# First loads of x and of the weights issued together on three queues, and the first squares on two engines, in an eight-core decoder layer

## The chip, the cores and the metric

The kernel runs on the 8 cores of one Trainium2 chip; every core works on one prompt and four sample rows. The metric is the time of the slowest core in device microseconds (us). Runs have a state: in the slow state one die (cores 0 to 3, or 4 to 7) has a clearly lower granted TensorE clock. Ratios and mean spans leave such runs out; a median of the table of runs is of all runs of that kernel, slow ones too. Small clock differences of a die remain; where they matter, the undisturbed cores are compared.

## The reference

One layer of a decoder. The part that this change touches is its very beginning, the first half-step FFN:

```python
def half_ffn(x, g, w_gate, w_up, w_down):
    h = rmsnorm(x, g)
    return (jax.nn.silu(h @ w_gate) * (h @ w_up)) @ w_down
...
xp = xp + 0.5 * half_ffn(xp, *ffn1)      # then attention, recurrence, memory, merge, second FFN
```

D_MODEL is 1024, D_FF is 2816, and a core has 2052 columns (tokens), cut into six tiles x0 to x5. Nothing can be multiplied before a tile's mean square is known, so the first matmuls wait for x, squares, a sum over 1024 rows and a scaling.

## The kernel before

Columns are tokens, rows are features: a tile x_k is 128 partitions x 8 chunks x n columns. Widths of the first three tiles are 352, 336 and 336.

```python
FT = [(0, 352), (352, 336), (688, 336), ...]      # first column, width

def load_x(k, src, parts=1, after=(), queues=(SP,)):
    w = 8 // parts                       # chunks in one DMA
    for q in range(parts):
        P.dma(queues[q % len(queues)], ... dst of chunks q*w .. , reads=list(after), writes=dx[k][q * w:(q + 1) * w])

def sq(k, c, late=1000.0, pair=True):    # first tiles: pair=False
    b = P.tile(brp)
    if not pair:
        actf(b, xv(k, c), AF.Square, [dx[k][c]], [b.d])                  # ScalarE
        mm(p, ones_n, b, c == 0, c == 7, ...)                            # sum over partitions, in PSUM
    ...
# rstd(k): Ln, then Exp on ScalarE -> 1/rms.   to_h(k, ...): hT = x * gain * rstd, 8 operations on VectorE

def gate_up(half, w, hook=None):
    for j in range(NJ):                                                  # 22 weight tiles of 128 x 2048
        b = load_w(w[j], 2048, first_w[min(j, 5)] if hook else ())       # on GpSimd's queue; waits for first_w
        for k in HT[half]:                                               # x0, x1, x2
            ... 8 matmuls gate, 8 matmuls up, Silu on ScalarE, product on VectorE

first_w = [dx[0][0:4], dx[0], dx[1][0:4], dx[1], dx[2][0:4], dx[2]]      # weight j waits for this part of x
```

The head of the program:

```python
load_x(0, xt, 4, queues=(SP, ACT))
... constants: ones_n, EPS, zero; then the gains (vecs, 128 rows of 208 bytes) on ScalarE's queue
for k in range(3):
    if k:
        load_x(k, xt, 2, after=dx[k - 1][0:5] if k == 1 else dx[k - 1][0:4])   # SyncE's queue only
    for c in range(8):
        sq(k, c, 0.0, False)
    to_h(k, rstd(k), gf1)
... four constants written by GpSimd (1.43 us), then gate_up(0, ...)
```

So x and weights take turns: x0, then w0 with x1, and so on. A list scheduler in the Python code decides, while the program is built, the order of instructions on each engine from a table of estimated costs (`DMA_RATE` is its estimate of each queue's rate). On the chip this order is fixed: an instruction that waits holds up everything behind it on its engine, ready or not (in e4 below, an Exp that was ready stood 8 us behind a square that was not).

The softmax here doesn't subtract the row's maximum and nothing guards it: scores larger than these inputs give would overflow.

## Time and profile before

| what | value |
|---|---|
| time, median of the first 3 runs | 1809.42 us (1807.29 to 1811.98) |
| slowest core of the profiled run | core 2, 1802.6 us |
| TensorE (PE) busy on it | 1738.2 us, 96% |
| matmuls in the first 60 us, by core 0 to 7 | 190, 166, 165, 190, 188, 175, 199, 169 (mean 180) |
| span + 0.143 us x that count, by core | 1825.8 to 1826.2 us |

A warm matmul of this stage starts 0.143 us after the one before it. Adding to each core's span the time of the matmuls that it finished in the first 60 us gives the same number for all eight cores within 0.4 us. So these cores differ only by what they did in the head, and a matmul gained there is 0.143 us gained at the end. I call the count N60.

The table by stretch for core 2, the slowest. In the brackets after each busy time is the number of instructions; the first bracket is TensorE's, and PEclk is the granted clock:

```profile
core 2: us, PE busy (x) PEld busy (x) DVE busy (x) ACT busy (x) POOL busy (x), PEclk, DMA share, GB/s
0.00:60.00 60.00, 33.07 (x165) 18.13 (x166) 16.16 (x35) 30.44 (x54) 7.33 (x20) 0.91 0.80 170
```

Core 2: 165 x 0.143 = 23.6 us of warm work in 60 us, so 36.4 us are lost. (The prediction below says 176 and 35: it added up windows of 5 us, which count a matmul that crosses a boundary twice. All counts from here on are of one window.)

The timeline of TensorE on core 2 (start, duration, operation, out<-in, count, and in brackets the idle time before it with what ended it). `hb` are the sums of squares, `ps` and `nd` the gate and up products; 352 columns is x0, 336 is x1 or x2:

```profile
10.27 3.80 PE L80 MATMUL hb<-br,cb 128*128 128x352 bf16 x8 [10.27 <-ACT br L80]
21.88 0.44 PE L80 MATMUL hb<-br,cb 128*128 128x336 bf16 x1 [7.81 <-ACT br L80]
...
23.06 0.79 PE L80 MATMUL ps<-hT,wp 128*128 128x352 bf16 x2
...
31.36 0.30 PE L80 MATMUL hb<-br,cb 128*128 128x336 bf16 x1 [3.67 <-ACT br L80]
...
43.58 0.72 PE L80 MATMUL ps<-hT,wp 128*128 128x336 bf16 x2 [3.79 <-DVE hT L80]
```

The first product (`ps`) comes at 23.06 us. What holds it back is the fixed order of ScalarE. There, the Exp that finishes 1/rms of x0 (the last line) stands behind a square of x1:

```profile
14.17 0.56 ACT L80 ACTIVATE fr<-hb,vec 128x352 f32<-128x352 f32 x1 [0.69 <-PE hb L80]
21.17 0.57 ACT L80 ACTIVATE br<-XA,vec 128x336 bf16<-128x336 f32 x1 [6.44 <-DMA XA<-xt]
21.65 0.57 ACT L80 ACTIVATE fr<-fr,vec 128x352 f32<-128x352 f32 x1
```

The Ln of x0 was done at 14.7 us, and w0 had landed at about 15.3 us (issued at 8.11, 7.2 us to landing); the Exp waited for x1. All eight cores show it: the Exp starts 0.5 us after that square (at 15.4 to 21.7 us), the first product 1.4 us after the Exp, and, by and large, the later x1 came, the smaller is the count of the core in the table above (199 on core 6, where x1 came first, 165 on core 2, where it came last).

Two matmuls in 0.59 us (23.06 to 23.65) is the slow rate; the Trainium skill (TensorE: Matmul & The Clock Gate, Part 1) tells of half rate until some 3.4 us of activity, and this trace agrees with 0.28 to 0.29 us a matmul after a long gap and 0.143 us once it is warm. The slow stretch from 43.58 us lasted 5.6 us here, with a granted clock of 0.50 in the records; in the first one, from 23.06 us, the records show 1.00, though the spacing is the same. The waits of TensorE on core 2 in the first 60 us (us in total, times, longest):

```profile
PE hb L80 <- ACT br L80: 22.9, 5, 10.3
PE ps L80 <- DVE hT L80: 3.8, 1, 3.8
```

ScalarE's squares are named, but they wait for x in their turn; the chain of waits of the same core says so (start, duration, what):

```profile
1.51 7.51 DMA XA<-xt
9.09 11.99 DMA XA<-xt
```

x0 took 7.5 us and x1 12.0 us. In the first 3 us of these 12 nothing of x1 moved, and then it shared the engines with w0 and w1. From 9 to 12 us almost nothing moved at all, as the DMA view of 9 to 12 us shows (queue, packets, MB written, share of the time of 16 DMA engines; q0 is GpSimd's weights, q1 SyncE's and q10 ScalarE's queue):

```profile
DMA packets 21, 0.09 MB, mean 29 GB/s; under 512 B 0, under 2 KB 0, under 8 KB 21
## 3 DMA queue, kind: packets, MB, share of 16 engines
q0 software_dynamic: 21, 0.09, 39.1%
```

### The profile page before, as it was taken

The page shows a single profiled execution, that of the slowest core. Times are in us where ns is not written, and L with a number is a line of the kernel's source. Part 1 is how long each engine was busy: PE and PEld are TensorE (multiplying, and loading weights), DVE is VectorE, ACT ScalarE, POOL GpSimd, SP SyncE. Part 2 cuts the span into 40 slices and gives each one's busy share as a digit, 9 for nine tenths or more (in the row PEclk, how much of TensorE's full clock was granted, in tenths as well). Part 3 has the DMA queues.
Part 4 walks back from the last instruction along what each step waited for, and adds up shares of the span by engine and source line. Part 5 has one row for each costly group of instructions (what it writes and reads, how often), then busy time and mean ns, then how long its engine had stood idle before and what let it go on. Part 6 is the DMA issues. An engine that isn't in the chain of part 4 may idle for free.

```text
span 1802.6 us, 33178 instructions; the slowest of 8 cores (1797.5 to 1802.6 us)
## 1 busy us (share of the span) xinstructions
PE 1738.2 (96%) x12105; PEld 1109.0 (62%) x12171; DVE 674.7 (37%) x1391; ACT 730.4 (41%) x1266; POOL 405.2 (22%) x543
## 2 busy tenths in 40 slices
PE   4999999999999999999999999999999999999996
PEld 1666666666655545555556566666666666666663
DVE  2223314222142435756576533543452221422213
ACT  5334414222145566758776633433342221322212
POOL 1112221001244051433431122322220002100021
PEclk9999999999999999999999999999999999999998
DMA  8486459656688554654547745596875447899562
GB/s 196 80 167 127 70 102 197 123 122 127 120 211 199 142 120 77 122 98 93 96 100 152 170 80 88 106 193 130 164 147 87 69 104 145 163 192 171 104 141 96
DMA packets 89391, 234.00 MB, mean 130 GB/s; under 512 B 32912, under 2 KB 40336, under 8 KB 86416
## 3 DMA queue, kind: packets, MB, share of 16 engines
q0 software_dynamic: 40608, 127.03, 44.6%
q1 hardware_dynamic: 46224, 59.26, 10.4%
q10 hardware_dynamic: 2400, 45.57, 8.7%
q8 instruction: 102, 1.67, 0.4%
q14 instruction: 57, 0.47, 0.1%
HBM read 321.27 MB, written 80.51 MB: 223 GB/s over the span
## 4 chain that ended last, share of the span: by engine, by line
PE 90%; DVE 3%; ACT 3%; issue 2%; DMA 1%; POOL 1%; DVEq 0%; ACTq 0%; SPq 0%; POOLq 0%
PE ps L80 49%; PE nd L80 33%; PE hb L80 8%; DVE XB L80 1%; ACT fr L80 1%; DMA XA<-xt 1%; DVE hT L80 1%; DVE br L80 1%; ACT br L80 0%; ACT L80 0%; ACT XA L80 0%; DVE fr L80 0%; POOL XA L80 0%; DVE XA L80 0%; POOL fr L80 0%
## 5 line engine op out<-in xcount | busy, mean ns | idle before, releaser
L80 PE MATMUL ps<-hT,wp 128*128 128x336 bf16 (+4 forms) x3839 | 637.2, 312 | 5.7 <-DVE hT L80 3.8
L80 PEld LDWEIGHTS ps<-hT,wp 128*128 128x128 bf16 x3856 | 365.6, 98 | 208.3 <-issue 6.4
L80 PE MATMUL nd<-hT,wp 128*128 128x336 bf16 (+4 forms) x2547 | 434.5, 312 | 1.4 <-ACT fr L80 0.2
L80 PEld LDWEIGHTS nd<-hT,wp 128*128 128x128 bf16 x2560 | 243.3, 98 | 134.7 <-issue 2.0
L80 ACT ACTIVATE fr<-ps,vec 128x336 f32<-128x336 f32 (+3 forms) x269 | 150.1, 560 | 343.8 <-PE ps L80 343.4
L80 PE MATMUL ps<-actb,wp 128*128 128x336 bf16 (+2 forms) x1612 | 253.8, 308 | 0.3 <-DVE XB L80 0.3
L80 PEld LDWEIGHTS ps<-actb,wp 128*128 128x128 bf16 x1612 | 157.3, 98 | 76.7 <-issue 0.6
L80 ACT ACTIVATE fr<-nd,vec 128x336 f32<-128x336 f32 (+3 forms) x185 | 103.4, 560 | 235.5 <-PE nd L80 235.2
L80 DVE TENSOR_TENSOR actb<-ps,fr 128x336 bf16<-128x336 f32 (+2 forms) x160 | 81.9, 514 | 266.2 <-PE ps L80 260.9
L80 PE MATMUL nd<-actb,wp 128*128 128x336 bf16 (+2 forms) x1076 | 173.0, 308 | 0.7 <-ACT fr L80 0.7
L80 POOL TENSOR_TENSOR fr<-fr 128x512 f32<-128x512 f32 (+3 forms) x96 | 108.0, 1132 | 161.0 <-DVE fr L80 140.2
L80 POOL DMA_DIRECT2D wp<-wgu x88 | 47.4, 538 | 400.3 <-PE ps L80 229.9
L80 PEld LDWEIGHTS nd<-actb,wp 128*128 128x128 bf16 x1076 | 105.0, 98 | 52.3 <-issue 1.0
L80 POOL TENSOR_TENSOR br<-fr 128x336 bf16<-128x336 f32 (+2 forms) x84 | 77.3, 923 | 181.2 <-ACT fr L80 181.0
L80 DVE TENSOR_TENSOR actb<-nd,fr 128x336 bf16<-128x336 f32 (+2 forms) x104 | 53.2, 513 | 173.2 <-PE nd L80 167.2
L80 ACT ACTIVATE fr<-XB,vec 128x352 f32<-128x352 f32 (+2 forms) x96 | 53.9, 577 | 138.5 <-DVE XB L80 138.5
L80 PE MATMUL hb<-hT,wp 128*128 128x512 bf16 (+1 forms) x514 | 95.2, 312 | 1.0 <-ACT fr L80 0.2
L80 ACT ACTIVATE fr<-XA,vec 128x336 f32<-128x336 f32 (+1 forms) x72 | 40.9, 578 | 130.2 <-DVE XA L80 130.2
L80 POOL DMA_DIRECT2D wp<-wd x64 | 34.8, 544 | 249.6 <-PE ps L80 128.5
L80 PE MATMUL hb<-br,cb 128*128 128x336 bf16 (+7 forms) x188 | 48.5, 300 | 28.9 <-ACT br L80 22.9
L80 ACT ACTIVATE fr<-fr,vec 128x512 f32<-128x512 f32 (+3 forms) x105 | 72.6, 700 | 5.0
L80 DVE SCALAR_TENSOR_TENSOR fr<-fr,ps 128x336 f32<-128x336 f32 (+2 forms) x85 | 43.2, 510 | 77.6 <-ACT fr L80 77.6
(244 smaller groups left out, 1630.9 us busy)
## 6 DMA issues: line engine op xcount, KB each, us to landing
wp<-wgu POOLq DMA_DIRECT2D x88, 512.0 KB, 8.9
wp<-wd POOLq DMA_DIRECT2D x64, 352.0 KB, 5.8
wp<-w_gb POOLq DMA_DIRECT2D x48, 384.0 KB, 8.8
wp<-w_hqf POOLq DMA_DIRECT2D x16, 512.0 KB, 8.3
vd<-br SPq DMA_DIRECT2D x48, 128.0 KB, 4.0
XA<-vd SPq DMA_DIRECT2D x12, 512.0 KB, 5.7
wp<-w_qk POOLq DMA_DIRECT2D x12, 512.0 KB, 7.6
pv<-fr SPq DMA_DIRECT2D x21, 256.0 KB, 6.4
```

The lines of the kernel that those rows point to most:

```text
L80: return f(*[g(x) for x in a], **{n: g(x) for n, x in k.items()})
```

## The change

The intent is to let nothing wait that need not: all of x0, x1 and x2 is issued at once on two queues, weights at once on the third, and squares go to whichever of ScalarE and VectorE the scheduler expects to be free. The scheduler gets one estimated rate for the first 20 us, 105 for every queue in place of 130 (SyncE), 190 (GpSimd) and 100 (ScalarE).

```diff
+    HEAD = 20000.0
+    HEAD_RATE = 105.0
...
-                    pipe[e] = max(pipe[e], start + issue) + o["nbytes"] / self.DMA_RATE[e]
+                    t = max(pipe[e], start + issue)
+                    pipe[e] = t + o["nbytes"] / (self.HEAD_RATE if t < self.HEAD else self.DMA_RATE[e])
...
+    def sq_first(k, c):
+        ...
+        P.op((ACT, DVE), (lambda e: e.activation(out=b.t[:, 0:n], in_=x, func=AF.Square, bias=zeroc, scale=1.0),
+                          lambda e: e.tensor_tensor(out=b.t[:, 0:n], in0=x, in1=x, op=ALU.mult)), reads=[dx[k][c], dc], writes=[b.d])
+        mm(p.t[:, 0:n], ones_n, b.t[:, 0:n], c == 0, c == 7, [b.d, dc], [p.d])
...
-            b = load_w(w[j].rearrange("p a c n -> p (a c n)"), 2048, first_w[min(j, 5)] if hook else ())
+            b = load_w(w[j].rearrange("p a c n -> p (a c n)"), 2048)
...
-    first_w = [dx[0][0:4], dx[0], dx[1][0:4], dx[1], dx[2][0:4], dx[2]]
...
-    load_x(0, xt, 4, queues=(SP, ACT))
+    P.dma(ACT, lambda e: e.dma_start(out=vec[:, 0:52], in_=vecs), writes=[dc])
+    for k in range(3):
+        load_x(k, xt, 4, queues=(SP, ACT))
...
-    P.dma(ACT, lambda e: e.dma_start(out=vec[:, 0:52], in_=vecs), writes=[dc])
     for k in range(3):
-        if k:
-            load_x(k, xt, 2, after=dx[k - 1][0:5] if k == 1 else dx[k - 1][0:4])
         for c in range(8):
-            sq(k, c, 0.0, False)
+            sq_first(k, c)
         to_h(k, rstd(k), gf1)
-    P.op(POOL, lambda e: e.memset(ones_b, 1.0), writes=[dm])      # and three more, moved to j == 5 of the weight loop
```

A part that adds filler matmuls in TensorE's idle time is in the diff as well, but it is never switched on (`fill` stays None).

More of the change, by code (lines that the diff above doesn't have):

```diff
@@ L183 @@
     WAIT = 1200.0
+    HEAD = 20000.0
+    HEAD_RATE = 105.0
+    fill, fill_end, FILL = None, 0.0, 80.0
     def __init__(self, nc, lanes=None):
@@ L384, in schedule @@
                 table = o["aset"]
+            if e == PE and order[PE] and self.fill is not None and start < self.fill_end:
+                o["fill"] = max(0, int((start - free[e] - 150.0) / self.FILL))
             o["t0"] = start
@@ L488, in body @@
                     for o in order[name]:
+                        for _ in range(o.get("fill", 0)):
+                            self.fill(e)
                         for s, k in o["waits"]:
@@ L722, in sq @@
             mm(p.t[:, 0:n], ones_n, b.t[:, 0:n], c == 1, c == 7, [b.d, dc], [p.d], late=late)
+    def sq_first(k, c):
+        n = FT[k][1]
+        if c == 0:
+            pss[k] = P.tile(psS)
+        p, b, x = pss[k], P.tile(brp), xv(k, c)
+        P.op((ACT, DVE), (lambda e: e.activation(out=b.t[:, 0:n], in_=x, func=AF.Square, bias=zeroc, scale=1.0),
+                          lambda e: e.tensor_tensor(out=b.t[:, 0:n], in0=x, in1=x, op=ALU.mult)), reads=[dx[k][c], dc], writes=[b.d])
+        mm(p.t[:, 0:n], ones_n, b.t[:, 0:n], c == 0, c == 7, [b.d, dc], [p.d])
     def rstd(k):
@@ L1359, in bulk_at @@
         return 1760e3
-    load_x(0, xt, 4, queues=(SP, ACT))
-    P.op(POOL, lambda e: e.memset(vec[:, 60:61], 1.0), writes=[d_one])
+    P.dma(ACT, lambda e: e.dma_start(out=vec[:, 0:52], in_=vecs), writes=[dc])
+    for k in range(3):
+        load_x(k, xt, 4, queues=(SP, ACT))
+    P.op(DVE, lambda e: e.memset(vec[:, 60:61], 1.0), writes=[d_one])
     P.op(ACT, lambda e: e.activation(out=vec[:, 63:64], in_=vec[:, 60:61], func=AF.Ln), reads=[d_one], writes=[d_one])
@@ L1367, in build_nc @@
     P.op(DVE, lambda e: e.memset(vec[:, 62:63], 0.0), writes=[dc])
-    P.dma(ACT, lambda e: e.dma_start(out=vec[:, 0:52], in_=vecs), writes=[dc])
     for k in range(3):
-        if k:
-            load_x(k, xt, 2, after=dx[k - 1][0:5] if k == 1 else dx[k - 1][0:4])
         for c in range(8):
-            sq(k, c, 0.0, False)
+            sq_first(k, c)
         to_h(k, rstd(k), gf1)
-    P.op(POOL, lambda e: e.memset(ones_b, 1.0), writes=[dm])
-    P.op(POOL, lambda e: e.memset(ones_h, 1.0 / 128), writes=[dm])
-    P.op(POOL, lambda e: e.memset(rst, 1.0), writes=[dm])
-    P.op(POOL, lambda e: e.memset(cb[:, 896:1408:64], 0.0), writes=[dm])
     for q, (src_, dst_) in enumerate(bulk):
@@ L1386, in hook @@
         elif j == 5:
+            P.op(POOL, lambda e: e.memset(ones_b, 1.0), writes=[dm])
+            P.op(POOL, lambda e: e.memset(ones_h, 1.0 / 128), writes=[dm])
+            P.op(POOL, lambda e: e.memset(rst, 1.0), writes=[dm])
+            P.op(POOL, lambda e: e.memset(cb[:, 896:1408:64], 0.0), writes=[dm])
             P.dma(ACT, lambda e: e.dma_start(out=cf[:, :], in_=cstf), reads=d_memT, writes=[dm])
```

## The prediction

> **What bounds the kernel now.** TensorE is busy 1738 of 1802.6 us (page, slowest core) and is 90% of the chain that ended last. The change touches only the first 45 us. There the timeline of core 2 shows the first ones-matmul at 10.3 us and the first real one at 23.06; the waits view puts 22.9 us on ACT squares (which wait for x) and 3.8 on hT. The windows table counts 176 matmuls in the first 60 us: at the warm spacing (0.143 us for 336 columns) 25 us of work, so 35 us were lost. Core 6 counts 208 (30 lost) and its span is 5.1 us shorter: head losses reach the end one for one. Cores 1, 2, 5, 7 all count 170 to 177. Part of the loss is clock: after a gap matmuls come 0.28 us apart for 4 to 6 us. The Trainium skill (TensorE: Matmul & The Clock Gate, Part 1) describes this, half rate until some 3.4 us of activity; the trace agrees.
>
> **Why the head is slow.** x and weights go in turn: w0 is issued at 8.1 us, x1 (two halves) at 9.1, only after x0, landing at 21.1 and 23.9; x2 at 21.1, landing at 28.8 and 32. From 9 to 12 us almost nothing moves (DMA windows). When busy, q0 writes 0.08 MB (reads 0.16) and q1 0.11 per us: 270 to 300 GB/s read.
>
> **What the change does.** All of x (4.19 MB) and seven weights (1.05 MB each) are issued from 1 us on. This adds no bandwidth: the Trainium skill (DMA: Bandwidth & Descriptors, Issuing engines are not separate DMA queues) says that they share 16 engines and interleave. The trace agrees: x1 needed 12 us while w0 and w1 ran. Estimate: x gets 155 GB/s of 270, so x0 lands later than now (8.5 us), at 12.5; w0 at 12.6, x1 21.5, w1 22, x2 30. After the last x0 squares come one more matmul, Ln, Exp and hT (0.56 us each): first real matmul at 16.5 instead of 23.1 us. Squares on two engines save about 1 us per tile, where the whole tile has landed. Moving POOL's memsets (1.43 us) lets weights go first. The filler code is never switched on. The changed rate only reorders instructions.
>
> **Sum, slow core.** Lost: 15.3 us around the first sums, 2.3 cold clock on w0 x0, 4 waiting for h of x1 (order is fixed in advance), 2.3 cold clock again, 0.5 other: 24.5 instead of 35.5 us. Gain 11 us; after 60 us nothing changes but small reordering (3 us either way).
>
> **Prediction.** 1809.4 - 11 = 1798 us, range 1791 to 1805. Faster by over 2%: 0.02; within 2%: 0.96; slower by over 2%: 0.02.
>
> **What shows it right or wrong.** x0 lands later than 8.6 us, first ps matmul between 14 and 18 us, hT of x2 complete before 37 us; matmuls in the first 60 us rise to about 245 on the slow cores, fewer at 0.28 us; the spread of cores shrinks. Windows from 100 us on look as before.
>
> **What would make it wrong.** If weights crowd out x (q0 started 4 us before q1 at 10 us although issued together), x0 lands at 15 us or later and the gain is 5. If the order fits the arrivals, the gain is 15. A reshuffle of the attention stage could add or take several us. Table switches (1.28 us) between Silu and Ln may stay in the chain of x1 and x2.

## The result, and the profile after

| | before | after |
|---|---|---|
| time of the first comparison, median of 4 | 1809.26 us (1807.29 to 1811.98) | 1804.57 us (1803.54 to 1805.91) |
| ratio of the fast runs | | 0.9973, 95% interval 0.9956 to 0.9991 |
| a second session on another chip, medians (of the fast runs alone 1805.51 and 1801.13) | 1805.79 us | 1801.27 us, ratio 0.9973 (0.9955 to 0.9991) |
| mean span of the eight cores there, fast runs | 1801.1 us | 1798.0 us |
| slowest core there, mean of the fast runs | 1804.2 us | 1799.6 us |
| N60 by core, profiled run | 165 to 199, mean 180 | 187 to 196, mean 191 (second session: 182 to 197, mean 192) |

A ratio is the mean time of one kernel's fast runs over that of the other's in the same rounds, so it is not quite the ratio of the medians.

The gain is 4.7 us where 11 were predicted, though the time itself lies in the predicted range. In the second session it splits into 3.1 us for the mean core and 1.5 us for a smaller distance from the mean core to the slowest. In the first comparison the cores 4 to 7 had a mean clock of 0.990 and were 3 to 4 us longer than their N60 says (core 0, at 0.992, 2 us); in the second they had 0.992 to 0.993 and only core 4 stood out, by 1.5 us. So that low clock is no steady part of the change.

The same views after, for core 4, the slowest of the profiled run (1802.0 us). By stretch:

```profile
core 4: us, PE busy (x) PEld busy (x) DVE busy (x) ACT busy (x) POOL busy (x), PEclk, DMA share, GB/s
0.00:60.00 60.00, 36.46 (x190) 20.13 (x191) 22.67 (x50) 23.41 (x41) 7.22 (x19) 0.89 0.79 170
```

The timeline of TensorE:

```profile
...
15.59 1.21 PE L80 MATMUL hb<-br,cb 128*128 128x352 bf16 x3 [4.76 <-ACT br L80]
18.69 4.85 PE L80 MATMUL ps<-hT,wp 128*128 128x352 bf16 x16 [1.89 <-DVE hT L80]
23.33 0.98 PE L80 MATMUL hb<-br,cb 128*128 128x336 bf16 x5
26.89 1.46 PE L80 MATMUL hb<-br,cb 128*128 128x336 bf16 x4 [2.58 <-ACT br L80]
31.47 1.47 PE L80 MATMUL hb<-br,cb 128*128 128x336 bf16 x4 [3.12 <-ACT br L80]
...
36.25 0.48 PE L80 MATMUL ps<-hT,wp 128*128 128x336 bf16 x1
```

The first product came 4.4 us earlier, at 18.69 us, 1.4 us after the Exp of x0 (17.27 us), which in the new order no longer stands behind a square of x1. But after w0 on x0 was done at 23.3 us, TensorE had only 15 sums to do until 36.25 us. Those sums are of x1 and of x2 alike: in the fixed order, all eight sums of x2 stand ahead of the products of x1. The waits:

```profile
PE hb L80 <- ACT br L80: 14.7, 6, 4.8
PE hb L80 <- DVE br L80: 6.9, 1, 6.9
PE ps L80 <- DVE hT L80: 1.9, 1, 1.9
```

ScalarE of the same core shows where the squares were (a line with [.. <-DMA XA<-xt] waited for x), with table loads and the Silu between them:

```profile
14.86 1.07 ACT L80 ACTIVATE br<-XA,vec 128x352 bf16<-128x352 f32 x2 [5.21 <-DMA XA<-xt]
...
26.18 1.04 ACT L80 ACTIVATE br<-XA,vec 128x336 bf16<-128x336 f32 x2 [5.25 <-DMA XA<-xt]
27.23 1.28 ACT L80 ACT_TABLE_LOAD   x1
28.53 0.55 ACT L80 ACTIVATE fr<-ps,vec 128x352 f32<-128x352 f32 x1
...
31.81 1.28 ACT L80 ACT_TABLE_LOAD   x1
33.11 0.54 ACT L80 ACTIVATE fr<-hb,vec 128x336 f32<-128x336 f32 x1
34.37 0.57 ACT L80 ACTIVATE br<-XA,vec 128x336 bf16<-128x336 f32 x1 [0.72 <-DMA XA<-xt]
34.85 0.56 ACT L80 ACTIVATE fr<-fr,vec 128x336 f32<-128x336 f32 x1
```

The last quarter of x0 reached ScalarE at 14.9 us (before, x0 was there at 9 us), that of x1 at 26.2 us, that of x2 at 34.4 us. The Exp of x1 (the last line) stood behind a square of x2. The chain of waits of the first 60 us on this core has one piece in place of the two of before:

```profile
4.58 29.71 DMA XA<-xt
```

And this is what the queues did from 10 to 12 us:

```profile
DMA packets 139, 0.45 MB, mean 223 GB/s; under 512 B 0, under 2 KB 0, under 8 KB 139
...
q0 software_dynamic: 47, 0.19, 59.0%
q10 hardware_dynamic: 47, 0.13, 22.8%
q1 hardware_dynamic: 45, 0.12, 21.3%
```

The three queues took turns packet by packet: 47, 47 and 45. The Trainium skill (DMA: Bandwidth & Descriptors, Queues, rings and completion order) says that each DMA engine goes round the queues "at *packet* granularity", and the counts agree. But the turns are not equally long. A weight packet held an engine for 0.590 x 16 x 2 us / 47 = 0.40 us, a packet of x (0.228 + 0.213) x 16 x 2 us / 92 = 0.153 us. So x, with two queues of three, had 44% of the engines' time and 0.125 MB per us, 125 GB/s.

### The profile page after: what moved, and what is told of

Read it like the earlier page. It is cut to its first block, busy times and chain, and to the rows that moved or that the text cites. A ratio compares the mean times of both kernels' runs of the same rounds, so it can differ in the third digit from the quotient of the medians.

```text
span 1802.0 us, 33181 instructions; the slowest of 8 cores (1797.7 to 1802.0 us)
## 1 busy us (share of the span) xinstructions
PE 1741.6 (97%) x12105; PEld 1109.3 (62%) x12171; DVE 681.7 (38%) x1404; ACT 722.9 (40%) x1252; POOL 404.5 (22%) x542
## 4 chain that ended last, share of the span: by engine, by line
PE 91%; DVE 3%; ACT 2%; issue 2%; DMA 2%; POOL 1%; ACTq 0%; DVEq 0%; POOLq 0%
PE ps L80 50%; PE nd L80 33%; PE hb L80 8%; DMA XA<-xt 2%; DVE XB L80 1%; ACT fr L80 1%; DVE br L80 1%; DVE hT L80 0%; ACT br L80 0%; ACT XA L80 0%; ACT L80 0%; DVE fr L80 0%; ACTq L80 0%; POOL XA L80 0%; DVE XA L80 0%
## 5 line engine op out<-in xcount | busy, mean ns | idle before, releaser
L80 PE MATMUL ps<-hT,wp 128*128 128x336 bf16 (+3 forms) x3829 | 633.9, 312 | 3.5 <-DVE hT L80 1.9
L80 PE MATMUL nd<-hT,wp 128*128 128x336 bf16 (+3 forms) x2557 | 435.3, 312 | 2.1 <-issue 0.9
L80 ACT ACTIVATE fr<-ps,vec 128x352 f32<-128x352 f32 (+3 forms) x276 | 154.0, 560 | 350.8 <-PE ps L80 350.5
L80 ACT ACTIVATE fr<-nd,vec 128x336 f32<-128x336 f32 (+3 forms) x178 | 99.6, 560 | 231.6 <-PE nd L80 231.1
L80 PE MATMUL hb<-br,cb 128*128 128x336 bf16 (+7 forms) x188 | 47.9, 305 | 27.8 <-ACT br L80 14.7
## 6 DMA issues: line engine op xcount, KB each, us to landing
wp<-wgu POOLq DMA_DIRECT2D x88, 512.0 KB, 10.4
```

Of the source, the lines that this page charges most:

```text
L80: return f(*[g(x) for x in a], **{n: g(x) for n, x in k.items()})
```

## The experiments

All kernels gave correct results. Every one was timed in 3 rounds against the kernel before; what is compared is the ratio, N60 and the arrival times. Two theories stood against each other:

- **Data.** Weights issued at once take the DMA engines from x, so x1 and x2 land late and TensorE starves.
- **Order.** The data would do, but the fixed order, made from a wrong estimate of rates, puts sums and squares of x2 ahead of the products and the Exp of x1.

| run | N60 mean (range) | median us | ratio to before (95%) |
|---|---|---|---|
| r1_after, the changed kernel | 192 (182 to 197) | 1801.27 | 0.9973 (0.9955 to 0.9991) |
| e1_order | 177 (173 to 182) | 1808.69 | 1.0014 (0.9998 to 1.003) |
| e3_weights_wait | 237 (221 to 247) | 1795.36 | 0.9941 (0.9925 to 0.9957) |
| e4_vecs_late | 181 (175 to 185) | 1801.96 | 0.9977 (0.9956 to 0.9999) |
| e2_act_squares | 181 (168 to 189) | 1801.91 | 0.9969 (0.9954 to 0.9984) |
| e5_old_order_held | 227 (213 to 235) | 1795.54 | 0.9935 (0.992 to 0.995) |
| e6_new_order_at_once | 201 (196 to 205) | 1798.54 | 0.9953 (0.9938 to 0.9968) |
| e9_best | 250 (243 to 263) | 1792.28 | 0.9917 (0.9901 to 0.9934) |
| e10_memsets_first | 188 (182 to 198) | 1807.25 | 0.9982 (0.9945 to 1.0018) |
| e11_best_held | 244 (239 to 249) | 1800.53 | 0.9928 (0.9907 to 0.9949) |
| e12_best_vecs_late | 260 (256 to 263) | 1804.52 | 0.9917 (0.9885 to 0.9949) |
| r2_best, e9_best again | 256 (243 to 262) | 1807.18 | 0.9928 (0.9908 to 0.9948) |

The last four lines need a warning: e10, e11, e12 and r2 ran in sessions in which cores 0 to 3 had a clock of 0.982 to 0.994 even in fast runs, and the kernel before took 1813.85 us (e10, e11) and 1821.27 us (e12, r2) there. Their medians are not to be set beside those above; the cores 4 to 7 of these sessions are, at 0.991 to 0.996 (in r2 cores 6 and 7 of the profiled run were still 5 us longer than their N60 says). Five of the medians include one or two slow runs; of the fast runs alone they are 1801.13 (r1), 1801.75 (e4), 1798.85 (e11), 1804.31 (e12) and 1806.30 us (r2).

### r1_after: the changed kernel again

> The changed kernel again, on the same chip as the next three. Every theory: ratio 0.997 to before; on the slow cores the second block of real matmuls (hT of x1) starts at 36 us, the last quarter of x0 lands at 14.7 us, the last of x2 at 34. It also shows whether the lower granted clock of die 1 (0.990 against 0.993) comes with the change or not: if it comes with the change, die 1 shows it here too and before doesn't.

Measured: N60 mean 192, ratio 0.9973, the same as the first time on another chip. The last squares of x0 began at 14.3 to 15.8 us, the first product at 18.2 to 19.7, the second block at 35.9 to 37.0 us. Die 1 had the clock of die 0 here, so its lower clock in the first comparison does not come with the change. One of its four runs was slow (2123 us).

### e1_order: the order alone

The scheduler is told rates nearer to the measured ones. The transfers stay as they are.

```diff
-    HEAD = 20000.0
-    HEAD_RATE = 105.0
+    HEAD = 36000.0
+    HEAD_RATE = {SP: 63.0, ACT: 63.0, POOL: 190.0}
...
```

> The changed kernel, with only the transfer rates that fix the instruction order made lower for x (63 GB/s on each of the two x queues for the first 36 us, 190 on the weights' queue), so that Exp of x1 stands ahead of the squares of x2 on ScalarE and the sums of x2 come after the first matmuls on hT of x1. Same transfers. Theory order (the wait for hT of x1 is made by the squares and sums of x2 placed ahead of it): landings unchanged (14.7, 26, 34 us), second block starts at 30 to 31 us instead of 36, 30 more matmuls in the first 60 us, 4 to 5 us faster than the changed kernel. Theory data (x arrives too late, whatever the order): second block still at about 36 us, no gain. Theory vecs: no gain.

Measured: a miss, and a useful one. The products of x1 did begin at 30.7 us in place of 36.3, as expected. But N60 fell to 177 and the ratio to before was 1.0014. The timeline of TensorE on core 4 shows a new wait in place of the old one:

```profile
30.68 0.44 PE L80 MATMUL ps<-hT,wp 128*128 128x336 bf16 x1 [3.40 <-DVE hT L80]
...
42.51 0.44 PE L80 MATMUL ps<-hT,wp 128*128 128x336 bf16 x1 [3.40 <-DVE hT L80]
```

hT of x2 was needed at 39 us and came at 42.5: its last squares (37.62 us) now stood behind two Silus and a table load on ScalarE, and its Ln (40.48 us) behind one more. The wait had only been moved to another place in the order. Some cores lost time much later as well. On core 7 the merge stage (1100 to 1300 us) waited for one weight, which the same core did not do in the profile of the changed kernel:

```profile
PE nd L80 <- DMA wp<-w_gb: 4.7, 1, 4.7
```

So this order, made for later arrivals, gave nothing while the arrivals stayed late. That no order could is not shown by it: part of the new wait is again order, and e6 below gains a little with late data.

### e3_weights_wait: the data alone, with a new order

x stays issued at once on two queues, and the rule `first_w` of before is put back, so weight 0 waits for the first half of x0 and so on.

```diff
-            b = load_w(w[j].rearrange("p a c n -> p (a c n)"), 2048)
+            b = load_w(w[j].rearrange("p a c n -> p (a c n)"), 2048, first_w[min(j, 5)] if hook else ())
+    first_w = [dx[0][0:4], dx[0], dx[1][0:4], dx[1], dx[2][0:4], dx[2]]
```

> The changed kernel, but each of the first six weights waits for the part of x that it waited for before the change (x is still issued at once). Theory data (the weights take the bandwidth that x needs): x0 lands at about 11 us instead of 14.7, x2 at about 22 instead of 34, second block of real matmuls at 25 to 27 us, 4 us or more faster than the changed kernel, although w0 lands later (15 to 17 us). Theory order: x2 lands earlier and so do its squares, so the wait behind them shrinks as well and the gain is about the same; the two are told apart by the run with the order alone. If SWDGE starts late and w0, w1 come too late, first real matmul at 20 us or more and no gain.

Measured: N60 237 and 1795.36 us, 5.9 us better than the changed kernel in the same session, and 10.4 us better than the kernel before. So x at once with the new order, without the weights at once, gave nearly the 11 us that were forecast for the whole change. With x alone in the queues, from 8 to 12 us on core 4:

```profile
q1 hardware_dynamic: 259, 0.62, 50.3%
q10 hardware_dynamic: 259, 0.64, 48.1%
```

That is 1.26 MB in 4 us, 315 GB/s for x instead of 125. The last squares of x0 began at 11.2 us (core 4) instead of 14.9. w0 came later, so the first product came later too, but products of x1 could follow at once:

```profile
20.84 1.06 PE L80 MATMUL ps<-hT,wp 128*128 128x352 bf16 x3
...
25.50 0.31 PE L80 MATMUL ps<-hT,wp 128*128 128x336 bf16 x1
```

The first product was 2.2 us later than in the changed kernel (w0 came later than the expected 15 to 17 us), the first of x1 10.7 us earlier. A gap of 13 us in the middle had been traded for 2 us at the start.

### e5_old_order_held and e6_new_order_at_once: the two crossed

In e3 the scheduler saw the waits, so the order changed too. These two runs separate that. In e5 the waits are added after the order is made, so that every engine has the changed kernel's order to the letter; in e6 the order is e3's to the letter and the waits are dropped afterwards.

```diff
         order = self.schedule()
+        for o in self.all:                         # e5: add the waits of the weights now
+            if o.get("hold"):
+                o["preds"] |= o["hold"]
+                o["t0"] += 1500.0
+            # e6 instead: o["preds"] -= o.get("drop", set())
```

> The instruction order of the changed kernel on every engine, kept to the letter, with the weights' issues held behind x as in e3_weights_wait (added after the order was made). So far span = 1825.1 us - 0.143 x (matmuls in the first 60 us) on every undisturbed core. Theory data: what counts is that x lands early; second block of real matmuls at 28 to 30 us instead of 36, 230 to 245 matmuls in the first 60 us (the changed kernel 192, e3_weights_wait 237), 1791 to 1797 us. Theory order: as the changed kernel, 185 to 200 matmuls, 1800 to 1802 us.

> The instruction order of e3_weights_wait to the letter, with all weights issued at once as in the changed kernel. Theory data: x2 lands at 34 us again, so about the changed kernel's loss: 185 to 205 matmuls in the first 60 us, 1799 to 1803 us. Theory order: as e3_weights_wait, 230 to 240 matmuls, 1794 to 1796 us.

Measured, N60 mean, and in brackets the mean span of the eight cores over the fast runs:

| | weights at once | weights wait for x |
|---|---|---|
| the changed kernel's order | 192 (1798.0 us) | 227 (1792.3 us) |
| e3's order | 201 (1796.5 us) | 237 (1791.5 us) |

Holding the weights is worth 35 or 36 matmuls in either order, that is 5.0 and 5.2 us by the count and 5.7 and 5.0 us by the spans. The order is worth 9 or 10 matmuls, 1.3 to 1.5 us by the count and 1.5 and 0.8 us by the spans. This settles the question between the theories: the weights that crowd x out are the main cause, the order a smaller one.

How small is less sure. The four kernels ran in two sessions (r1 and e3 on one chip, e5 and e6 on another, both undisturbed). Set against the mean span of the kernel before in the same session (1801.1 and 1801.7 us), holding is worth 6.3 and 4.3 us and the order 2.1 and 0.1 us. And in e6 GpSimd writes its constants first, so its weights start 1.3 us later than in the changed kernel and x0 and x1 land some 2 us earlier; so a part of what the first column puts down to the order may be data.

The gap that matters is the one between the products of x0 and of x1. In e5, in the changed kernel's order to the letter, it lies on core 4 between these lines:

```profile
26.12 2.11 PE L80 MATMUL hb<-br,cb 128*128 128x336 bf16 x9
...
32.51 0.48 PE L80 MATMUL ps<-hT,wp 128*128 128x336 bf16 x1
```

That is 6.39 us with 15 sums in it, so 4.2 us are lost, where the changed kernel with the weights at once lost 10.8. The expectation for e5 was a little too high: the second block began at 30.5 to 32.5 us instead of 28 to 30, and N60 is 227 instead of 230 to 245. e6 fell in the range of theory Data by N60 (185 to 205) and half a us below it in time (1799 to 1803).

In e5 the price of holding is plain to see. The waits of TensorE on core 4 in the first 60 us:

```profile
PE ps L80 <- DMA wp<-wgu: 8.4, 1, 8.4
...
PE hb L80 <- ACT br L80: 5.4, 6, 1.8
```

The squares of ScalarE are hardly waited for any more (5.4 us in place of 14.7), and the wait has become one for w0, 8.4 us. It is the smaller evil.

### e2_act_squares: the squares on ScalarE alone

```diff
-            sq_first(k, c)
+            sq(k, c, 0.0, False)
```

> The changed kernel, with the squares of the first tiles back on ScalarE alone. All theories of mine hold that the second engine for squares is worth little: squares are 0.49 us each and wait for data. 175 to 200 matmuls in the first 60 us, within 3 us of the changed kernel (1799 to 1804 us). If squares on two engines carry the gain of the change, it falls back to 165 to 180 matmuls and 1804 us or more.

Measured: N60 181 instead of 192, mean span 1799.0 instead of 1798.0 us, the ratio the same within its interval. By these numbers squares on two engines are worth about 1 us (1.6 us by the count, 0.4 us when each span is set against the kernel before in its own session). The order changed with it (products of x1 began at 29.4 us, but one at a time between sums), so this is the sum of both.

### e4_vecs_late: the small packets behind x0

The changed kernel issues `vecs`, 128 rows of 208 bytes, as the first transfer on ScalarE's queue, ahead of its half of x0. On core 4 of the changed kernel, 3 to 4 us, they take the turns of queue q10:

```profile
q1 hardware_dynamic: 116, 0.30, 90.3%
q10 hardware_dynamic: 112, 0.02, 10.7%
```

In 112 packets q10 moved 0.02 MB, and q1 0.30 MB of x in as many. The experiment issues them after x0 and gives the constants their own dependence.

```diff
-    P.dma(ACT, lambda e: e.dma_start(out=vec[:, 0:52], in_=vecs), writes=[dc])
-    for k in range(3):
-        load_x(k, xt, 4, queues=(SP, ACT))
+    load_x(0, xt, 4, queues=(SP, ACT))
+    ... constants, writes=[dz]
+    P.dma(ACT, lambda e: e.dma_start(out=vec[:, 0:52], in_=vecs), reads=[dz], writes=[dc])
+    for k in (1, 2):
+        load_x(k, xt, 4, after=[dz], queues=(SP, ACT))
```

> The changed kernel, but the small load of the gain vectors (128 rows of 208 bytes) is issued on the ACT queue after the two parts of x0 there, as before the change, with the constants on a dependence of their own. Theory vecs (128 small packets take one turn each in the round of the queues and push the last quarter of x0 back by the length of one x part): the last square of x0 starts at 10 to 11.5 us instead of 14.9, the first real matmul at about 15 instead of 18.7; hT of x1 still late at 35 to 36 us, so 0 to 2 us faster at most. Rival (the weights alone delay x0): x0 still at 14 us or later.

Measured: the last squares of x0 began at 10.8 to 12.7 us instead of 14.4 to 14.9 (14.3 to 15.8 in r1, the same session), so the direction was right and the size at the small end. But the first product, expected at about 15 us, came at 23.1 to 24.3, N60 was 181 instead of 192, and the time did not move (ratio 0.9977; mean span 1799.6 instead of 1798.0 us). ScalarE of core 4 shows why:

```profile
14.14 0.55 ACT L80 ACTIVATE fr<-hb,vec 128x352 f32<-128x352 f32 x1 [0.69 <-PE hb L80]
22.41 0.57 ACT L80 ACTIVATE br<-XA,vec 128x336 bf16<-128x336 f32 x1 [7.72 <-DMA XA<-xt]
22.89 0.57 ACT L80 ACTIVATE fr<-fr,vec 128x352 f32<-128x352 f32 x1
```

The scheduler had put a square of x1 between the Ln (14.14) and the Exp (22.89) of x0. x1 landed at 22.4 us, and x0, ready for 8 us, waited for it. It is the same trap as in the kernel before: the earlier x0 could not be used.

### e10_memsets_first: GpSimd's constants back in front

```diff
+    P.op(POOL, lambda e: e.memset(ones_b, 1.0), writes=[dm])      # and three more, before gate_up again
```

> The changed kernel with one part undone: POOL writes its four constants between the first weight issues again, as before the change, instead of after them; PE, ACT, DVE and SP keep their order to the letter. The first weight is issued as early as in the changed kernel or a fraction of a us later, the second and third some 1.4 us later. Theory data (what counts is how many weights are in the queues beside x): x0's last square ends at 13.0 to 14.3 us instead of 14.9, the first real matmul comes at 17 to 18.2 us instead of 18.7, the second block stays at 35 to 36.5 us because the order is fixed; 190 to 202 matmuls in the first 60 us, ratio to before 0.995 to 0.998. Rival (moving the constants was a part of the gain, because weights come earlier): PE waits for a weight in the first block, under 187 matmuls, ratio 0.998 to 1.001.

Measured: theory Data missed; the rival's numbers nearly came (ratio 0.9982), but not its reason. On the undisturbed cores 4 to 7 N60 was 182 to 189 with a mean of 186 (expected 190 to 202, or under 187), TensorE waited for no weight on core 4, and the last squares of x0 began at 14.6 to 15.0 us, no earlier than before. The scheduler put the memsets between the weight issues and left w0 at 1.58 us, against 1.55 us in the changed kernel. The cores 4 to 7 were 3.1 us shorter than those of the kernel before in the same session, in r1 3.0 us, so moving the constants is worth nothing that can be seen. For x0 it seems to matter that w0 is in the queue, not whether w1 follows a little later; e9 and e11 agree.

### e9_best: x at once, w0 at once, the others held, and more work for x0

The experiments pointed to this: hold the weights except w0, whose lateness was e5's new wait, and use x0 for the first three weights before x1 is needed. The scheduler gets rates between the two of above.

```diff
-    HEAD = 20000.0
-    HEAD_RATE = 105.0
+    HEAD = 30000.0
+    HEAD_RATE = {SP: 85.0, ACT: 85.0, POOL: 150.0}
...
+    first_w = [(), dx[0][0:4], dx[0], dx[1], dx[2][0:4], dx[2]]
...
+            groups = [list(range(3))] + [[j] for j in range(3, NJ)]
+        for js in groups:
+            for k, j in [(k, j) for k in HT[half] for j in js]:      # x0 with w0, w1, w2; then x1 with them; then x2
```

> Built from both: x at once, w0 at once, w1 to w5 held behind parts of x; the first three weights all run on x0 before x1 is needed; and the rates that fix the order set to what was seen (85 GB/s on each x queue for 30 us, 150 on the weights' queue). If both data and order matter: w0 on x0 from about 16.5 us, w1 and w2 on x0 fill the wait for hT of x1, 260 to 290 matmuls in the first 60 us, 1784 to 1789 us. If only data matters: as e3_weights_wait, 1794 to 1796.

Measured: N60 250 and 1792.28 us, below the expected 260 to 290 and above the expected time, but the fastest kernel of an undisturbed session, with a ratio of 0.9917. It beats the kernel before by 14.9 us in its own session and, across sessions, the changed one by 9.0 us. What is missing is that x0 still landed late (last squares at 14.5 to 14.9 us), as w0 alone is enough to take every third turn (46 packets of the weights' queue, 46 and 43 of the queues of x from 10 to 12 us on core 4).

### e11_best_held: w0 held as well

```diff
-    first_w = [(), dx[0][0:4], dx[0], dx[1], dx[2][0:4], dx[2]]
+    first_w = [dx[0][0:4], dx[0], dx[1][0:4], dx[1], dx[2][0:4], dx[2]]
```

> The best kernel so far (250 matmuls in the first 60 us, 1792.3 us) with one rule changed: the first weight too waits for the first half of x0, as before the change. Theory data: x0's last square ends at 11 to 12 us instead of 14.7; w0 lands at about 20 us, so x0's first block starts at 19.5 to 21 us instead of 18 to 19, and what x gains w0 loses: 240 to 262 matmuls, 1790 to 1794 us, the same within 0.2 per cent. Rival (x0's arrival is what bounds the head whatever the weights do): over 265 matmuls, under 1789 us. If holding w0 costs more than it gives: under 238 matmuls, over 1794 us.

(The edit moves w1 and w2 back by half a tile of x as well.) Measured: as theory Data expected. x0's last squares began at 11.0 to 11.7 us, 3.4 us earlier, and the first product at 20.1 to 21.4 us, 2.3 us later: TensorE now waits for w0 (8.6 us on core 5). On the undisturbed cores 4 to 7 N60 is 242 to 247 and the span 1790.0 us in the mean; e9's cores 4 to 7 had 245 to 249 and 1789.2 us. What x gains w0 loses. The median of 1800.53 us, outside the expected range, comes from the disturbed die, and one of its five runs was slow.

### e12_best_vecs_late and r2_best: the small packets once more, with an order that can use them

e12 is e9 with the edit of e4; here the order on ScalarE keeps Ln and Exp of x0 together. r2 is e9 again in the same session.

> The best kernel so far (1792.3 us, 250 matmuls in the first 60 us) with one more edit, the one that was tried alone before: the 128 small packets of the constants go after x0 on ScalarE's queue and the constants have a dependence of their own; the order on ScalarE keeps Ln and Exp of x0 ahead of the squares of x1. x0's last square starts at 10.8 to 12.5 us instead of 14.7, the first real matmul at 15 to 17 us instead of 18.5, if w0 has landed. Theory (x0's arrival at 14.7 costs what it is late): 258 to 280 matmuls in the first 60 us, 1788 to 1791 us. Rival (the sum of what has to land bounds the head, so that an earlier x0 is paid for by a later w1 or x1): 243 to 256 matmuls, 1791 to 1793.5 us.

> The best kernel so far once more, on the same chip as the run beside it, so that the two are compared in one session: 243 to 256 matmuls, 0.990 to 0.993 of before.

Measured: x0's last squares at 11.0 to 12.3 us instead of 14.7 to 15.0, the first product at 16.9 to 17.8 us, which is later than expected, and N60 260 against 256. So 3 us of an earlier x0 became 4 matmuls, half a us, at the lower end of what the theory expected. The cores 4 to 7 took 1791.3 us in the mean of the fast runs, r2's 1790.7 (the times expected of e12, 1788 to 1793.5 us over both theories, can be held only against these cores). The two cannot be told apart by time.

## Why the prediction was right and where it was wrong

**Right: the place, and that x lands later.** Only the first 60 us changed in earnest. Span plus 0.143 us x N60 is 1825 us or a little more for the undisturbed cores of the changed kernel, 1826 for before. The queues share the DMA engines and interleave, as the Trainium skill has it (DMA: Bandwidth & Descriptors, Issuing engines are not separate DMA queues): x0 landed later than before, not earlier. The spread between cores shrank.

**Right for another reason: the earlier first product.** The prediction put the late start of before down to x and w0 going in turn. But w0 had landed there at about 15.3 us; the first product waited for the Exp of x0, which stood behind a square of x1 on ScalarE. In the changed order it does not, and so the first product came earlier although x0 landed 6 us later. No run tried that order alone in the kernel before. An estimate from core 2: with the Exp at 14.7 us, when the Ln was done, and the first product 1.4 us later, it would have come at about 16 us instead of 23.06.

**Wrong: the wait between the products of x0 and of x1.** The sum, with what core 4 measured (one window; a matmul counts 0.143 us):

| term of the sum | predicted lost us | measured lost us | how |
|---|---|---|---|
| up to the first product | 15.3 | 17.4 | first product at 18.69, 9 sums of 0.143 us before it |
| slow clock on w0 x0 | 2.3 | 2.4 | 16 matmuls 0.290 us apart |
| "4 waiting for h of x1 (order is fixed in advance)" | 4 | 10.8 | from 23.33 to 36.25 us, less 15 sums |
| slow clock again | 2.3 | 2.1 | 15 matmuls 0.285 us apart, to 40.5 us |
| other | 0.5 | 0.1 | the rest |
| sum | 24.5 | 32.8 | 60 - 190 x 0.143 = 32.8 |

The step that failed is the third term, the wait for h of x1. It took 10.8 us and not 4, which is 6.8 of the 8.3 us by which the sum is short; the first product (18.69 instead of 16.5 us) is another 2.1 us. The third term failed through an earlier step, the estimate "x gets 155 GB/s of 270". The total was estimated too low rather than too high: from 10 to 12 us x received 125 GB/s and weights 95 GB/s as written, which are 190 GB/s as read (32 bits in, 16 out), 315 GB/s together, as much as x alone got in e3. It was the share that was wrong. The prediction gave x 57% of the bytes; it got 40%, because the queues share turns and a weight packet's turn is 2.6 times as long. With that x1 landed at 26.2 us and x2 at 34.4 us instead of 21.5 and 30.

The late x0 has another cause as well. In e4, with the same weights at once and only `vecs` moved behind x0, the last squares of x0 began at 10.8 to 12.7 us, about where the prediction had x0 (12.5); in e3, with `vecs` in front but the weights held, at 10.9 to 11.7. So it takes both, the weights and the small packets in front, to make it 14.9, and the prediction does not mention the small packets.

The prediction knew that the order is fixed but did not ask what stands between the products of x0 and of x1 in it. Here sums and squares of x2 did, so that x2's arrival at 34.4 us, not x1's at 26.2, set the start of x1. The crossed runs show which counts: in this same order with the weights held (e5), the third term is 4.2 us, as forecast. By them the data is worth 4 to 6 us, the order 0 to 2 us. A caution belongs to this: in e1 a new order by itself only moved the wait from x1 to x2.

**The marks that it set.** x0 landing later than 8.6 us: right. First product between 14 and 18 us: 18.3 to 18.7, just outside. hT of x2 complete before 37 us: wrong, on core 4 VectorE worked on hT of x1 and then of x2 from 35.5 to 43.3 us. About 245 matmuls in the first 60 us: the same way of counting (5 us windows) gives 201 for core 4. Fewer matmuls at 0.28 us: right, some 31 in two stretches against some 40 in three, by the spacings in the two timelines. Cores closer together: right. The stretches after 100 us as before: right, apart from the clock.

**The risk that it named.** "If weights crowd out x [...] x0 lands at 15 us or later and the gain is 5" is what happened: last squares of x0 at 14.9 us, gain 4.7. It was listed as what would make the prediction wrong and not given enough weight, though the profile of before had the evidence: x1 took 12.0 us beside w0 and w1, x0 7.5 us mostly alone. That the time still lies in the stated range, by 0.4 us, is due to its width.

**What stays open.** Why some runs of the changed kernel had a clock of 0.990 on one die is not known; the second session did not show it. The waits in the merge stage in e1 were seen and not explained. The difference of about 2.6 us between e12's cores 4 to 7 and what their N60 lets one expect arose after 1500 us: core 5 had 20 matmuls fewer left there than in r2 (1859 against 1879, as many as it had gained in the head), yet ended only 0.7 us earlier, at a clock of 0.96 against 0.98; why the clock was lower is not known. And nobody ran the kernel before with the Exp of x0 ahead of the squares of x1, nor one kernel with each part of the change alone, so the 4.7 us are not divided among the parts.

## What to carry to other kernels

Issuing everything at once gained 4.7 us here, and holding the weights back gained 5.9 us more: what is issued at once gives away the say over what arrives first, and the queue with the longest packets (0.40 against 0.153 us) took 59% of the engines' time. Hold back what is not needed yet and let what everything waits for go alone; then check, in the fixed order of each engine, that nothing waiting for a late tile stands in front of work for an early one. And count in one window: matmuls finished in the head, times their warm spacing, told the span of almost every undisturbed core within half a us (e1 and e12 excepted), which no percentage of busy time would have.

## What the Trainium skill lacked or had wrong

- DMA: Bandwidth & Descriptors, Queues, rings and completion order: it says that an engine goes round the queues packet by packet, which the counts confirm (47, 47, 45 in 2 us). It does not say that turns are then unequal in time and bytes: a casting weight packet (32 to 16 bits) held an engine 0.40 us, a packet of x 0.153 us, so x with two queues of three got 44% of the engines' time and 125 GB/s, against 315 GB/s alone.
- The same page, Issuing engines are not separate DMA queues: right about interleaving. It says of several issuing engines only that they save issue time. The section on queues lets one infer that a further queue takes turns from those already running; what this costs neither section says. With w0 on the third queue ahead of x0's landing, x0's last squares came at 14.5 to 14.9 us instead of 11.0 to 11.7 (e9 against e11).
- ScalarE: Activation LUTs, What ACT_TABLE_LOAD costs: the load of some 1283 ns agrees (1.28 us). The drain of 1380 ns that the page adds to every switch does not show here: on core 4 of the changed kernel the square ended at 27.22 us and the Silu began at 28.53, 1.31 us for the whole switch.
- No page has a figure for small packets ahead of large ones in the same queue: 128 rows of 208 bytes in front of half of x0, with weights in the third queue, cost x0 some 2 to 4 us (last squares at 10.8 to 12.7 us without, 14.4 to 14.9 with).
